# A hybrid decoder layer: TensorE's order stated by hand too, transfers in the account of outstanding work, the solve's tiles in another pool, three short products ahead of the branch projections

## The chip, the cores and the metric

The kernel runs on one core of a Trainium2 chip. The metric is the device time of one execution in microseconds (us). Engine names as in the profile: PE is TensorE's matmul, PEld its weight load, DVE VectorE, ACT ScalarE, POOL GpSimd, SP the engine that issues the weights' transfers.

## The reference, cut to what matters

One decoder layer on a sequence of 256 positions of width 2048, all in float32, eight heads of 128 in each of two branches, and a gated feed-forward part of width 5632.

```python
h = rms_norm(x, ln1)
proj = h @ w_in                     # q, k, v, beta, decay, z of A; q, k, v of B; two gates
y_a = gated_deltanet(...) @ w_branch_a       # causal conv 4, l2norm, chunks of 64,
                                             # triangular solve per chunk, state scan, norm
y_b = moba_attention(rope(q_b), rope(k_b), v_b) @ w_branch_b   # block 256: causal attention here
merged = sigmoid(gate_a) * y_a + sigmoid(gate_b) * y_b
x = x + merged @ w_out
h = rms_norm(x, ln2)
u = causal_dwconv(h @ w_up, ffn_conv, ffn_conv_bias)           # width 3
u_gate, u_val = split(u)
x = x + (silu(u_gate) * u_val) @ w_down
out = rms_norm(x, final_norm)
```

## The kernel before

Activations lie transposed, 128 features on the partitions and 256 positions in a row. Each large product is made of three: a value is split into a high and a low part of a reduced float32 type, and for each block of 128 input features TensorE multiplies `wh` by the high part, `wh` by the low part and `wl` by the high part. That triple, of 256 columns each, is what `block` writes through `main_mm` (L168). A piece of weights comes by a transfer of 1 MB into `wraw`; ScalarE casts 1024 columns of it to `wh`, VectorE subtracts to get `wl`. Such 1024 columns are called a half here: 24 products. Four buffers of halves are there, and halves are counted from the start of the program: the gates' projections (`ps_gate`) lie in halves 112 to 175, the branches (`ps_br`) in 176 to 207, the output projection (`ps_wo`) in 208 to 239, the up projection (`ps_up`) from 240, the down projection (`pd`) behind 416.

Beside the large products of the input projection run the two branches, written as generators ("jobs"): `decay`, the gated DeltaNet with its triangular solve, the rotary part and the attention. Each time 1700 ns worth of large products have been written (16 products), `main_mm` calls `tick()`, which lets each job go on to its next `yield` if an account of outstanding work permits it: `Metered` adds a number for each operation that it issues on ScalarE and VectorE to `load`, a tick takes `EVERY` off, no job steps while `load` is above `ROOM`, and `ready` holds a job back until its last operations should be done. What has to wait longer says `yield from wait(n)`, a fixed number of ticks. `quick` holds the jobs of the projections' own results, `bg` the background ones.

From the first projection on, `manual_schedule` states that DVE, ACT and POOL take their instructions in the order in which they are written. TensorE is not among them: its order is put together by a scheduler with a model of its own. `order_st.close()` ends the stated order behind the gates.

Names that return below: `posi` and `ang` (positions and angles), `cs`, `dS`, `CS` (cosines and sines and their way through DRAM), `X_` and `Xc` (the rotated quarter of queries and keys, fetched by POOL's transfers), `sc` and `s_` (scores), `pT` (transposed weights of the attention); in the DeltaNet `ssq`, `pvt`, `dA`, `X`, `Xa`, `tm`, `W`, `Xr` (the solve), `py`, `Y`, `pu`, `r`, `w`, `z`, `g`, `po`, `pot` (short products behind it, of 128 columns and less). `g` is the pool of the solve's tiles, on the right side of the memory; it is freed when `early` has four entries, and the gates' results take its place. `gl` is the pool of what lives longer. A `kick` (L275) is three dummy products of 128 columns ahead of a chunk, named in `KICKS`.

Of the kernel before, what the change touches and what calls it, by code (L numbers as in the profile page):

```python
# [11 lines left out]
F32 = mybir.dt.float32  # L12
# [18 lines left out]
TABLE = 1220  # L31
TABLES = (AF.Exp, AF.Sigmoid, AF.Silu, AF.Sqrt, AF.Sin)
# [3 lines left out]
KICKS = {"gate": (7,), "up": (1, 23)}  # L36
# [39 lines left out]
def layer_kernel(ctx: ExitStack, tc: tile.TileContext, w_first, xT, pos, cst, vec, convw, ffw, bdv,  # L76
                 w_gdn, w_bd, w_moba, w_mv, w_gate, w_ba, w_bb, w_o, w_up, w_dn, fnorm, out):
    nc = tc.nc
    pe, pool, sp = nc.tensor, nc.gpsimd, nc.sync

    class Metered:
# [5 lines left out]
        def __getattr__(self, op):  # L87
            f = getattr(self.eng, op)

            def run(*args, **kw):  # L90
                n = max([a.free_size() for a in (*args, *kw.values()) if hasattr(a, "free_size")], default=0)
                if op == "reciprocal":
                    n *= 6
                if op == "dma_start":
                    n = 0
                func = [a for a in (*args, *kw.values()) if isinstance(a, type(AF.Exp)) and a in TABLES]
                extra = TABLE if func and func[0] != self.table else 0
                self.table = func[0] if func else self.table
                met(self.name, n * self.per + self.each, extra)
                return f(*args, **kw)  # L100

            return run

    act, dve = Metered(nc.scalar, "act", 0.87, 110), Metered(nc.vector, "dve", 1.03, 60)
# [13 lines left out]
    quick, bg, load, clock, ready = [], [], {"dve": 0.0, "act": 0.0}, [0.0], {}  # L118
# [147 lines left out]
    def chunk(x, kt, name, steps=((0, 0, None), (1, 0, None)), c=None):  # L266
        ps = mmt("ps_" + name)
        ws = {}
        if kt == H:
            ws = dict.fromkeys(range(2), take())  # L270
        if c in KICKS.get(name, ()):
            ws[0] = take()
            idle = sdt("kick")
            for _ in range(3):
                pe.matmul(idle[:, :P], ws[0][1][0][0][:, :P], x.one(0, 0)[:, :P], start=True, stop=True)  # L275
# [155 lines left out]
    gl_st = ExitStack()  # L431
    gl = gl_st.enter_context(tc.tile_pool(name="gl", bufs=2, reuse_waits="tile"))
# [3 lines left out]
    dr = gdn_st.enter_context(tc.tile_pool(name="dr", bufs=2, space=bass.MemoryType.DRAM))  # L436
# [3 lines left out]
    def rotary():  # L440
        while not left:
            yield
        posi = m.tile([P, 32], I32, name="posi", tag="pT_")
        sp.dma_start(posi, pos)
        ang = m.tile([P, 32], F32, name="ang", tag="s_")
        with late():
            dve.tensor_copy(ang, posi)
        dve.tensor_scalar(ang, ang, C["invf"], None, op0=ALU.mult)
        qn = m.tile([P, 32], F32, name="qn", tag="s_")
        MAGIC = 1.5 * 2 ** 23  # L450

# [36 lines left out]
        dve.tensor_scalar(ang, ang, 3.1415925, -3.1415925, op0=ALU.min, op1=ALU.max)  # L488
        cs = m.tile([P, 2, 32], F32, name="cs_", tag="s_")
        act.activation(cs[:, 1], ang, AF.Sin)  # L490
        act.activation(cs[:, 0], ang, AF.Sin, scale=0.5)
        yield
        dve.tensor_tensor(cs[:, 0], cs[:, 0], cs[:, 0], op=ALU.mult)
        dve.tensor_scalar(cs[:, 0], cs[:, 0], -2.0, 1.0, op0=ALU.mult, op1=ALU.add)
        for a in range(2):
            for j in range(2):
                pool.dma_start(dram(dS, a * 32 * T + j * T, (2 * T, 16), (1, T)), cs[:, a])
        yield from wait(2)
        for a in range(2):
            pool.dma_start(CS[:, a], dram(dS, a * 32 * T, (0, 2), (P, 64), (1, P)))  # L500
        turned.append(True)


    def decay():
# [38 lines left out]
        dve.tensor_scalar(rem, gc[:, :P], gc[:, P - 1:P], -1.0, op0=ALU.subtract, op1=ALU.mult)  # L543
        left.append(rem)
# [18 lines left out]
    left, early, ended, joined, turned, seen = [], [], [], [], [], []  # L563
# [57 lines left out]
    def gdn(h0, kq, v):  # L621
# [53 lines left out]
        yield from wait(2)  # L675
# [19 lines left out]
        yield  # L695
        vb = gl.tile([P, 2, 2, P], F32, name="vb")
# [12 lines left out]
        yield from wait(2)  # L709
# [4 lines left out]
        yield from wait(2)  # L714
# [3 lines left out]
        for i in range(1, 16):  # L718
            tm = g.tile([P, 2, 2, 16], F32, name="tm", tag="tm", bufs=1)
# [15 lines left out]
        def rows(dst, w, a, neg):  # L735
            tm = g.tile([P, 2, 16, 16], F32, name="tw", tag="tm", bufs=1)
# [4 lines left out]
        W = g.tile([P, 2, 16], F32, name="W", bufs=1)  # L741
        rows(W, X0, r3(Xa[:, :512], 32)[:, :, 16:], True)
        yield
        Xr = g.tile([P, 16, 16], F32, name="Xr", bufs=1)
        pool.dma_start(Xr.rearrange("p m c -> p (m c)"), dram(dX, 0, (256, 16), (0, 8), (1, 256)))
        yield from wait(5)
# [6 lines left out]
        yield from wait(2)  # L753
# [7 lines left out]
        yield from wait(2)  # L761
# [5 lines left out]
        yield from wait(2)  # L767
        Et = gl.tile([P, 2, 32], F32, name="Et", bufs=1)
        dve.transpose(Et, E[:, 0])
        yield from wait(2)  # L770
# [8 lines left out]
        yield from wait(2)  # L779
# [3 lines left out]
        yield  # L783
        for j in range(2):
# [10 lines left out]
        for i in range(2):  # L795
# [11 lines left out]
            yield from wait(2)  # L807
# [5 lines left out]
            if i == 0:  # L813
# [8 lines left out]
                yield from wait(2)  # L822
# [19 lines left out]
        yield from wait(2)  # L842
# [8 lines left out]
    def moba(h0, q, k, v):  # L851
# [12 lines left out]
        yield from wait(4)  # L864
# [6 lines left out]
        yield from wait(4)  # L871
# [35 lines left out]
        yield from wait(2)  # L907
# [3 lines left out]
        yield from wait(2)  # L911
# [13 lines left out]
        yield from wait(2)  # L925
# [16 lines left out]
    def delta(gr):  # L942
# [5 lines left out]
        if gr == 0:  # L948
            order_st.enter_context(tc.manual_schedule(engines={
                mybir.EngineType.DVE, mybir.EngineType.Activation, mybir.EngineType.Pool}))  # L950
            load.update(dve=2400.0, act=0.0)
# [80 lines left out]
    while len(early) < 4:  # L1032
        tick()
# [3 lines left out]
    more = gp.tile([P, 14, 2, T], F32, name="gts")  # L1037
    gts += [more[:, c] for c in range(14)]
# [229 lines left out]
```

## Time and profile before

| | us |
|---|---|
| three runs: lowest, median, highest | 1468.44, 1473.16, 1473.19 |
| the profiled execution | 1473.24 |
| its span | 1471.4 |
| PE, DVE, ACT, POOL busy | 1449.4, 963.4, 767.0, 187.1 |
| idle of DVE just ahead of `wl` | 379.8 |
| idle of ACT just ahead of `wh` | 559.9 |

The execution lasts 1.8 us longer than the span that the profile covers. The profile cuts the span into stages by time: the input projection with the two branches beside it lies from the start to about 485, the remaining gates to 563, the branch projections to 654, the output projection to 744, the up projection to 1224 and the down projection behind it. A row's releaser is the operation that ended the wait. Products overlap in the records, so the duration of a single one (0.28 us alone) is longer than the distance between two; the distance is read from a stretch of many in the chain of work.

### The profile page before, as it was taken

The page shows a single profiled execution, that of the slowest core. Times are in us where ns is not written, and L with a number is a line of the kernel's source. Part 1 is how long each engine was busy: PE and PEld are TensorE (multiplying, and loading weights), DVE is VectorE, ACT ScalarE, POOL GpSimd, SP SyncE. Part 2 cuts the span into 40 slices and gives each one's busy share as a digit, 9 for nine tenths or more (in the row PEclk, how much of TensorE's full clock was granted, in tenths as well). Part 3 has the DMA queues.
Part 4 walks back from the last instruction along what each step waited for, and adds up shares of the span by engine and source line. Part 5 has one row for each costly group of instructions (what it writes and reads, how often), then busy time and mean ns, then how long its engine had stood idle before and what let it go on. Part 6 is the DMA issues. An engine that isn't in the chain of part 4 may idle for free.

```text
span 1471.4 us, 26958 instructions
## 1 busy us (share of the span) xinstructions
PE 1449.4 (99%) x11268; PEld 1390.0 (94%) x11268; DVE 963.4 (65%) x1385; ACT 767.0 (52%) x1093; POOL 187.1 (13%) x236
## 2 busy tenths in 40 slices
PE   9998999999999999999999999999999999999998
PEld 9988899999999999999999999999999998888886
DVE  7785869686755645766776666666666666644454
ACT  7654556656565544444555554545555554444444
POOL 0003131223210300100131111111111110000000
PEclk9999999999999999999999999999999999999999
DMA  8555565656355555566586555555555555555553
GB/s 310 173 180 160 178 207 184 203 172 224 126 190 178 184 190 183 181 220 205 196 246 216 197 201 192 187 196 200 191 188 196 201 188 185 200 200 192 186 195 114
DMA packets 46457, 283.80 MB, mean 193 GB/s; under 512 B 7632, under 2 KB 8800, under 8 KB 14464
## 3 DMA queue, kind: packets, MB, share of 16 engines
q1 hardware_dynamic: 39344, 270.38, 53.1%
q0 software_dynamic: 6272, 9.61, 2.5%
q8 instruction: 88, 1.44, 0.4%
q10 hardware_dynamic: 720, 2.10, 0.4%
q14 instruction: 33, 0.27, 0.1%
HBM read 275.34 MB, written 3.82 MB: 190 GB/s over the span
## 4 chain that ended last, share of the span: by engine, by line
PE 93%; DVE 3%; ACT 2%; DMA 1%; issue 1%; POOL 0%; ACTq 0%; DVEq 0%; POOLq 0%
PE ps_up L168 33%; PE pd L116 16%; PE ps_gate L168 12%; PE ps_wo L168 6%; PE ps_br L168 6%; PE ps_gdn L168 6%; PE ps_moba L168 5%; PE ps_v L168 2%; PE ps_z L168 2%; PE ps_gdn L341 2%; DVE wl L100 1%; ACT wh L100 1%; ACT L100 0%; PE g L116 0%; DMA dS<-cs__1202 0%
## 5 line engine op out<-in xcount | busy, mean ns | idle before, releaser
L100 DVE TENSOR_TENSOR wl<-wraw,wh 128x1024 fp32r<-128x1024 f32 (+1 forms) x496 | 612.6, 1238 | 379.8 <-ACT wh L100 378.7
L100 ACT CAST wh<-wraw 128x1024 fp32r<-128x1024 f32 (+1 forms) x496 | 514.5, 1042 | 559.9 <-PE ps_up L168 195.5
L168 PE MATMUL ps_up<-h,wh 128*128 128x256 f32 x2816 | 479.5, 276 | 0.0
L168 PEld LDWEIGHTS ps_up<-h,wh 128*128 128x128 f32 x2816 | 424.1, 188 | 0.0
L168 PE MATMUL ps_up<-h,wl 128*128 128x256 f32 x1408 | 389.2, 276 | 0.0
L168 PEld LDWEIGHTS ps_up<-h,wl 128*128 128x128 f32 x1408 | 264.3, 188 | 0.0
L168 PE MATMUL ps_gate<-hc,wh 128*128 128x256 f32 x1024 | 181.7, 281 | 1.5 <-ACT wh L100 1.5
L168 PEld LDWEIGHTS ps_gate<-hc,wh 128*128 128x128 f32 x1024 | 156.4, 189 | 1.9 <-ACT wh L100 1.9
L168 PE MATMUL ps_gate<-hc,wl 128*128 128x256 f32 x512 | 143.4, 280 | 1.9 <-DVE wl L100 1.9
L116 PE MATMUL pd<-wl,ah 128*128 128x512 f32 x336 | 125.5, 389 | 0.0
L116 PE MATMUL pd<-wh,al 128*128 128x512 f32 x336 | 124.4, 389 | 0.0
L116 PE MATMUL pd<-wh,ah 128*128 128x512 f32 x336 | 115.6, 389 | 0.0
L168 PE MATMUL ps_gdn<-hc,wh 128*128 128x256 f32 x640 | 115.0, 283 | 0.0
L1132 POOL TENSOR_TENSOR acts<-sg,cvf 128x256 f32<-128x256 f32 x44 | 62.7, 1426 | 408.3 <-ACT sg L100 400.0
L168 PEld LDWEIGHTS ps_gdn<-hc,wh 128*128 128x128 f32 x640 | 99.5, 192 | 0.5 <-issue 0.4
L168 PEld LDWEIGHTS ps_gate<-hc,wl 128*128 128x128 f32 x512 | 96.1, 188 | 2.3 <-DVE wl L100 2.3
L168 PE MATMUL ps_gdn<-hc,wl 128*128 128x256 f32 x320 | 91.0, 286 | 6.5 <-DVE wl L100 6.5
L168 PE MATMUL ps_moba<-hc,wh 128*128 128x256 f32 x512 | 90.2, 279 | 2.3 <-ACT wh L100 2.3
L168 PE MATMUL ps_wo<-mc,wh 128*128 128x256 f32 x512 | 90.5, 281 | 0.0
L168 PEld LDWEIGHTS ps_moba<-hc,wh 128*128 128x128 f32 x512 | 77.6, 188 | 2.6 <-ACT wh L100 2.5
L168 PEld LDWEIGHTS ps_wo<-mc,wh 128*128 128x128 f32 x512 | 78.6, 190 | 0.0
L116 PEld LDWEIGHTS pd<-wh,ah 128*128 128x128 f32 x336 | 63.1, 188 | 13.1
(405 smaller groups left out, 1981.8 us busy)
## 6 DMA issues: line engine op xcount, KB each, us to landing
wraw<-in_w_up SPq DMA_DIRECT2D x88, 1024.0 KB, 4.9
wraw<-in_w_dn SPq DMA_DIRECT2D x44, 1024.0 KB, 4.9
wraw<-in_w_gate SPq DMA_DIRECT2D x32, 1024.0 KB, 4.9
wraw<-in_w_gdn SPq DMA_DIRECT2D x28, 1024.0 KB, 5.2
wraw<-in_w_moba SPq DMA_DIRECT2D x16, 1024.0 KB, 4.9
wraw<-in_w_o SPq DMA_DIRECT2D x16, 1024.0 KB, 4.9
wraw<-in_w_mv SPq DMA_DIRECT2D x8, 1024.0 KB, 5.0
wraw<-in_w_ba SPq DMA_DIRECT2D x8, 1024.0 KB, 4.8
```

What stands on the lines that cost most here:

```text
L100: return f(*args, **kw)
L116: pe.matmul(ps, a, b, start=(start and i == 0), stop=(stop and i == n - 1), **kw)
L168: mark[0] = pe.matmul(ps, a, b, start=start, stop=stop, skip_group_check=True).ins
L341: pe.matmul(ps_two[b // 2][:, b % 2], wv[t][:, k - a, b * P:(b + 1) * P], hc.one(k, x_), start=(k == t == x_ == b % 2 == 0), stop=(k == KD ...
L1132: pool.tensor_tensor(acts[:, c, :], sg, t[:, 1, :], op=ALU.mult)
```

## The change

It has four parts. TensorE joins the engines whose order is the written one, and the stated order ends behind the last gates. POOL gets an account too (`Metered`, `ISSUE` = 560 for each transfer), and `yield "land"` stands where a job waits for a transfer: its next step is not taken ahead of the clock plus POOL's account plus `LAND` = 5200. A tick is still gated by DVE and ACT alone. Several waits become a single `yield`; the load of `posi` is issued by POOL, no longer by SP. The solve's tiles (`X`, `Xa`, `tm`, `W`, `Xr`) and the DRAM pool go to `gl`; `g` is freed when `clear` has four entries, behind the transposes `pvt`. The gates' results are split: eleven in the place of `g`, three in a pool `gq` that opens when `gl` and `m` are closed. And a kick stands ahead of the first branch chunk.

```diff
+ISSUE = 560
+MORE = 11
+LAND = 5200
-KICKS = {"gate": (7,), "up": (1, 23)}
+KICKS = {"gate": (7,), "br": (0,), "up": (1, 23)}
...
-                    n = 0
+                    n = ISSUE
...
+    pool = Metered(nc.gpsimd, "pool", 1.0, 0)
...
+    def landed():
+        return clock[0] + load["pool"] + LAND
+
     def step(jobs, it):
         old = dict(load)
-        if next(it, bg) is bg:
+        said = next(it, bg)
+        if said is bg:
             jobs.remove(it)
-        ready[id(it)] = clock[0] + max([load[e] for e in load if load[e] > old[e]], default=0.0)
+        ready[id(it)] = clock[0] + max([load[e] for e in ("dve", "act") if load[e] > old[e]], default=0.0)
+        if said == "land":
+            ready[id(it)] = max(ready[id(it)], landed())
...
-                if max(load.values()) < most and ready.get(id(it), 0.0) <= clock[0] + soon_:
+                if max(load["dve"], load["act"]) < most and ready.get(id(it), 0.0) <= clock[0] + soon_:
...
         if c in KICKS.get(name, ()):
-            ws[0] = take()
+            ws[0] = ws.get(0) or take()
...
-        sp.dma_start(posi, pos)
+        pool.dma_start(posi, pos)
+        yield "land"
...
-        yield from wait(2)
+        yield "land"
         for a in range(2):
             pool.dma_start(CS[:, a], dram(dS, a * 32 * T, (0, 2), (P, 64), (1, P)))
...
+        clear.append(h0)
...
+        while 2 * len(early) < h0:
+            yield
-        X = g.tile([P, 160], F32, name="X", bufs=1)
+        X = gl.tile([P, 160], F32, name="X", bufs=1)
         pool.tensor_copy(X, C["rows"])
-        yield from wait(2)
+        yield "land"
...
-        Xa = g.tile([P, 33 * 32], F32, name="Xa", bufs=1)
+        Xa = gl.tile([P, 33 * 32], F32, name="Xa", bufs=1)
         pool.dma_start(Xa[:, :1024], dram(dC, 0, (1024, 16), (0, 8), (1, 1024)))
-        yield from wait(4)
+        yield "land"
...
-        yield from wait(2)
+        there = landed()
         py = r3(sdt("py")[:, :64], 32)
...
+        while clock[0] < there:
+            yield
...
         each(lambda t, b, o: pool.dma_start(X_[o, b], t))
-        yield from wait(4)
+        yield "land"
...
         each(lambda t, b, o: pool.dma_start(t, Xc[o, b]))
-        yield from wait(4)
+        yield "land"
...
             order_st.enter_context(tc.manual_schedule(engines={
-                mybir.EngineType.DVE, mybir.EngineType.Activation, mybir.EngineType.Pool}))
+                mybir.EngineType.DVE, mybir.EngineType.Activation, mybir.EngineType.Pool,
+                mybir.EngineType.PE}))
...
-    while len(early) < 4:
+    while len(clear) < 4:
         tick()
     gdn_st.close()
...
-    for c in range(2, 16):
+    for c in range(2, 2 + MORE):
         gate(c, gts[c])
     while quick or bg:
         tick()
-    order_st.close()
     m_st.close()
     gl_st.close()
+    gq = y_st.enter_context(tc.tile_pool(name="gq", bufs=1, side="right", reuse_waits="tile"))
+    last = gq.tile([P, 14 - MORE, 2, T], F32, name="gtl")
+    gts += [last[:, c] for c in range(14 - MORE)]
+    for c in range(2 + MORE, 16):
+        gate(c, gts[c])
+    flushed(quick)
+    order_st.close()
...
-        join(bts[0], chunk(yc[0], H, "br"), gts[c])
+        join(bts[0], chunk(yc[0], H, "br", c=2 * c), gts[c])
```

Three places of the resulting order. First VectorE around the first rotation. `cs` is the last step of the cosines and sines, whose transfers `Xc` depends on; `un` and `kq` are steps of a projection's own convolution; each `wl` is one half. Before:

```order
L100 TENSOR_TENSOR cs__1202<-cs__1202 128x32
L100 TENSOR_SCALAR cs__1202<-cs__1202 128x32
L100 SCALAR_TENSOR_TENSOR aq_1226<-g_1119,st,gam 128x256 x2
L100 TENSOR_TENSOR wl<-wraw,wh 128x1024 x4
L100 TENSOR_TENSOR Xc<-X__1308,CS 128x256
L100 TENSOR_TENSOR Xs<-X__1308,CS 128x128 x2
L100 TENSOR_TENSOR Xc<-Xc,Xs 128x128 x2
L100 TENSOR_TENSOR un<-ps_gdn,R_415 128x512
L100 TENSOR_TENSOR wl<-wraw,wh 128x1024 x2
```

Now, from `cs` on, the first rows, and behind them the rows up to `Xc`, with five more `wl` in between:

```order
L103 TENSOR_TENSOR cs__1358<-cs__1358 128x32
L103 TENSOR_SCALAR cs__1358<-cs__1358 128x32
L103 TENSOR_TENSOR un<-ps_gdn,R_415 128x512
L103 TENSOR_TENSOR wl<-wraw,wh 128x1024 x2
L103 SCALAR_TENSOR_TENSOR kq<-un,cwv,kq 128x255
```

```order
L103 SCALAR_TENSOR_TENSOR kq<-un,cwv,kq 128x253
L103 TENSOR_TENSOR wl<-wraw,wh 128x1024
L103 TENSOR_TENSOR Xc<-X__1289,CS 128x256
L103 TENSOR_TENSOR Xs<-X__1289,CS 128x128 x2
L103 TENSOR_TENSOR Xc<-Xc,Xs 128x128 x2
```

Between `cs` and `Xc` stood four `wl`, now eight, and `un` has moved from behind `Xc` to the place right behind `cs`. The scores' products `sc` of this job stood in TensorE's row at half 42.04, with their first reader on VectorE ahead of the `wl` of half 42; now at half 47.33, with the reader ahead of the `wl` of half 51.

Second, TensorE around the last `pot`, the DeltaNet's last short product, in the gates. Before, at half 147.33:

```order
L168 MATMUL ps_gate<-hc,wl 128x256
L168 MATMUL ps_gate<-hc,wh 128x256 x2
L846 MATMUL pot<-ct,ot 128x128 x4
L168 MATMUL ps_gate<-hc,wl 128x256
L168 MATMUL ps_gate<-hc,wh 128x256 x2
```

Now, at half 150.67:

```order
L178 MATMUL ps_gate<-hc,wl 128x256
L178 MATMUL ps_gate<-hc,wh 128x256
L862 MATMUL pot<-ct,ot 128x128 x4
L178 MATMUL ps_gate<-hc,wh 128x256
L178 MATMUL ps_gate<-hc,wl 128x256
```

`pot` has moved down by three and a third halves, and it stands behind one `wh` product of its triple where it stood behind two.

Third, a short product with its operand, as the changed order has them: TensorE around `pu`, at half 64.00, and VectorE around `Y`, which `pu` reads. The `wl` rows ahead of and behind `Y` are those of halves 66 and 67.

```order
L178 MATMUL ps_gdn<-hc,wh 128x256 x2
L178 MATMUL ps_gdn<-hc,wl 128x256
L796 MATMUL pu<-E,Y 128x32 x2
L178 MATMUL ps_gdn<-hc,wh 128x256 x2
L178 MATMUL ps_gdn<-hc,wl 128x256
```

```order
L103 TENSOR_TENSOR wl<-wraw,wh 128x1024
L103 TENSOR_TENSOR Y<-py,ct 128x256
L103 TENSOR_TENSOR s__2528<-sc,ct 128x384
L103 TENSOR_REDUCE mx<-s__2528 128x1 x2
L103 TENSOR_SCALAR mx<-mx 128x2
L103 TENSOR_TENSOR un<-ps_gdn,R_415 128x512
L103 TENSOR_TENSOR wl<-wraw,wh 128x1024
```

In the changed order such short products stand only where a tick was, that is at multiples of 16 products, two thirds of a half.

More of the change, by code (lines that the diff above doesn't have):

```diff
@@ L78, in layer_kernel @@
     nc = tc.nc
-    pe, pool, sp = nc.tensor, nc.gpsimd, nc.sync
+    pe, sp = nc.tensor, nc.sync
     class Metered:
@@ L116, in mmg @@
             pe.matmul(ps, a, b, start=(start and i == 0), stop=(stop and i == n - 1), **kw)
-    quick, bg, load, clock, ready = [], [], {"dve": 0.0, "act": 0.0}, [0.0], {}
+    quick, bg, load, clock, ready = [], [], {"dve": 0.0, "act": 0.0, "pool": 0.0}, [0.0], {}
     def met(name, n, more=0.0):
         load[name] += n + more
+    def landed():
+        return clock[0] + load["pool"] + LAND
     def step(jobs, it):
         old = dict(load)
-        if next(it, bg) is bg:
+        said = next(it, bg)
+        if said is bg:
             jobs.remove(it)
-        ready[id(it)] = clock[0] + max([load[e] for e in load if load[e] > old[e]], default=0.0)
+        ready[id(it)] = clock[0] + max([load[e] for e in ("dve", "act") if load[e] > old[e]], default=0.0)
+        if said == "land":
+            ready[id(it)] = max(ready[id(it)], landed())
     def tick():
@@ L431, in layer_kernel @@
     gl_st = ExitStack()
+    dr = gl_st.enter_context(tc.tile_pool(name="dr", bufs=2, space=bass.MemoryType.DRAM))
     gl = gl_st.enter_context(tc.tile_pool(name="gl", bufs=2, reuse_waits="tile"))
@@ L435, in layer_kernel @@
     gdn_st = ExitStack()
-    dr = gdn_st.enter_context(tc.tile_pool(name="dr", bufs=2, space=bass.MemoryType.DRAM))
     g = gdn_st.enter_context(tc.tile_pool(name="g", bufs=2, side="right", reuse_waits="tile"))
@@ L561, in turned_out @@
         dve.tensor_scalar(cols[:, 0:2, :].rearrange("p a b -> p (a b)"), pt[:, :32], -1.0, None, op0=ALU.mult)
-    left, early, ended, joined, turned, seen = [], [], [], [], [], []
+    left, early, ended, joined, turned, seen, clear = [], [], [], [], [], [], []
     order_st = ExitStack()
@@ L708, in gdn @@
             pool.dma_start(dC[8 * e:8 * e + 8], dram(dA, e * 32 * (P + 1), (64 * (P + 1), 8), (P, 32), (1, 32)))
-        yield from wait(2)
-        Xa = g.tile([P, 33 * 32], F32, name="Xa", bufs=1)
+        yield "land"
+        Xa = gl.tile([P, 33 * 32], F32, name="Xa", bufs=1)
         pool.dma_start(Xa[:, :1024], dram(dC, 0, (1024, 16), (0, 8), (1, 1024)))
-        yield from wait(4)
+        yield "land"
         pool.memset(r3(Xa, 33)[:, :, 0:1], -1.0)
-        yield from wait(2)
+        yield
         Xd = X.rearrange("p (e x) -> p e x", e=2)[:, :, :64].rearrange(
@@ L718, in gdn @@
         for i in range(1, 16):
-            tm = g.tile([P, 2, 2, 16], F32, name="tm", tag="tm", bufs=1)
+            tm = gl.tile([P, 2, 2, 16], F32, name="tm", tag="tm", bufs=1)
             dve.tensor_tensor(tm[:, :, :, :i + 1], Xd[:, :, :, :i + 1],
@@ L735, in rows @@
         def rows(dst, w, a, neg):
-            tm = g.tile([P, 2, 16, 16], F32, name="tw", tag="tm", bufs=1)
+            tm = gl.tile([P, 2, 16, 16], F32, name="tw", tag="tm", bufs=1)
             dve.tensor_tensor(tm, w[:, :, None, :].to_broadcast([P, 2, 16, 16]),
@@ L739, in rows @@
             dve.tensor_reduce(dst, tm, axis=AX.X, op=ALU.add, negate=neg)
-        W = g.tile([P, 2, 16], F32, name="W", bufs=1)
+        W = gl.tile([P, 2, 16], F32, name="W", bufs=1)
         rows(W, X0, r3(Xa[:, :512], 32)[:, :, 16:], True)
-        yield
-        Xr = g.tile([P, 16, 16], F32, name="Xr", bufs=1)
+        yield "land"
+        Xr = gl.tile([P, 16, 16], F32, name="Xr", bufs=1)
         pool.dma_start(Xr.rearrange("p m c -> p (m c)"), dram(dX, 0, (256, 16), (0, 8), (1, 256)))
-        yield from wait(5)
+        yield "land"
         rows(Xm, W, Xr, False)
@@ L752, in gdn @@
         early.append(h0)
-        yield from wait(2)
+        yield "land"
         E = gl.tile([P, 2, 2, 32], F32, name="E", bufs=1)
@@ L760, in gdn @@
                            dram(dA, j * (P + 1) * P + 64, (P, 64), (2 * (P + 1) * P, 2), (1, 64)))
-        yield from wait(2)
+        yield "land"
+        Et = gl.tile([P, 2, 32], F32, name="Et", bufs=1)
+        dve.transpose(Et, E[:, 0])
         for b in range(2):
@@ L766, in gdn @@
             yield
[L767 to L770, printed above, removed]
+        there = landed()
         py = r3(sdt("py")[:, :64], 32)
@@ L778, in gdn @@
                           r3(C["mb"], 32)[:, None].to_broadcast([P, 2, 4, 32]), op=ALU.mult)
-        yield from wait(2)
+        yield
         pu = r3(sdt("pu")[:, :64], 32)
@@ L783, in gdn @@
         yield
+        while clock[0] < there:
+            yield
         for j in range(2):
@@ L806, in gdn @@
             dve.tensor_tensor(vb[:, i, 1], vb[:, i, 1], pz, op=ALU.subtract)
-            yield from wait(2)
+            yield
             p1_ = sdt("w1")[:, :P]
@@ L821, in gdn @@
                         dve.tensor_tensor(vb[o, 1, b], vb[o, 1, b], pr[64 * b:64 * b + 64, j, :], op=ALU.subtract)
-                yield from wait(2)
+                yield
         ended.append(h0)
@@ L841, in gdn @@
             act.mul(ot[:, p], po[:, p], st[:, 7, p:p + 1])
-        yield from wait(2)
+        yield
         pot = r3(sdt("pot"), T)
@@ L863, in moba @@
         each(lambda t, b, o: pool.dma_start(X_[o, b], t))
-        yield from wait(4)
+        yield "land"
         dve.tensor_tensor(Xc, X_, CS[:, 0:1, :].to_broadcast([P, 2, P]), op=ALU.mult)
@@ L870, in moba @@
         each(lambda t, b, o: pool.dma_start(t, Xc[o, b]))
-        yield from wait(4)
+        yield "land"
         ss, pss, mxs = [], [], []
@@ L906, in moba @@
         exps(1)
-        yield from wait(2)
+        yield
         share(0)
@@ L910, in moba @@
         share(1)
-        yield from wait(2)
+        yield
         pps = []
@@ L924, in moba @@
             ss[j] = pT
-        yield from wait(2)
+        yield
         py = r3(sdt("py_b"), T)
@@ L949, in delta @@
             order_st.enter_context(tc.manual_schedule(engines={
-                mybir.EngineType.DVE, mybir.EngineType.Activation, mybir.EngineType.Pool}))
-            load.update(dve=2400.0, act=0.0)
+                mybir.EngineType.DVE, mybir.EngineType.Activation, mybir.EngineType.Pool,
+                mybir.EngineType.PE}))
+            load.update(dve=2400.0, act=0.0, pool=0.0)
             bg.append(decay())
@@ L1036, in layer_kernel @@
     gp = y_st.enter_context(tc.tile_pool(name="gp", bufs=1, side="right", reuse_waits="tile"))
-    more = gp.tile([P, 14, 2, T], F32, name="gts")
-    gts += [more[:, c] for c in range(14)]
-    for c in range(2, 16):
+    more = gp.tile([P, MORE, 2, T], F32, name="gts")
+    gts += [more[:, c] for c in range(MORE)]
+    for c in range(2, 2 + MORE):
         gate(c, gts[c])
```

## The prediction

> **What bounds the kernel now.** I read the page first, for the engines' shares of the span. Quoted are the span and the busy times (us, share of the span, instructions).
>
> ```profile
> span 1471.4 us, 26958 instructions
> PE 1449.4 (99%) x11268; PEld 1390.0 (94%) x11268; DVE 963.4 (65%) x1385; ACT 767.0 (52%) x1093; POOL 187.1 (13%) x236
> ```
>
> TensorE is busy for 1449.4 of 1471.4 us, and the change takes no product out of it. So there are two kinds of gain: the 22 us in which it is not busy, and the time that its own products take. The view of busy time by stretches finds both; its columns are the stretch, its length, then busy time and instructions of PE, PEld, DVE, ACT and POOL, the granted clock, the DMA share and GB/s.
>
> ```profile
> 60.00:100.00 40.00, 39.68 (x253) 34.20 (x252) 33.33 (x76) 24.33 (x32) 1.46 (x2) 1.00 0.49 165
> 100.00:165.00 65.00, 55.77 (x420) 53.83 (x419) 46.01 (x104) 32.84 (x51) 16.31 (x28) 0.92 0.52 167
> 165.00:395.00 230.00, 229.01 (x1874) 222.12 (x1873) 176.54 (x358) 140.92 (x254) 58.50 (x105) 1.00 0.58 192
> 395.00:415.00 20.00, 16.62 (x135) 15.71 (x134) 10.17 (x20) 12.96 (x30) 7.32 (x13) 1.00 0.36 115
> ```
>
> TensorE idles 0.32, 9.23, 0.99 and 3.38 us in these four, 13.9 us together, nearly all of it at 100 to 165 and 395 to 415. Only in the second is the granted clock below 1.00. What it waits for comes from the view of waits (us in total, times, longest), of TensorE in 100 to 165, in 395 to 415, and one row of 165 to 480; then of VectorE in 60 to 480.
>
> ```profile
> PE ps_gdn L168 <- DVE wl L100: 6.5, 5, 3.0
> PE ps_moba L168 <- ACT wh L100: 2.3, 1, 2.3
> ...
> PE ps_gate L168 <- DVE wl L100: 1.9, 2, 1.1
> PE ps_gate L168 <- ACT wh L100: 1.5, 2, 1.2
> ...
> PE pT L916 <- DVE s__2575 L100: 0.7, 1, 0.7
> ```
>
> ```profile
> DVE Xc L100 <- DMA X__1308<-qk: 7.6, 1, 7.6
> DVE s__4831 L100 <- PE sc L876: 6.9, 1, 6.9
> DVE s__1521 L100 <- PE sc L876: 6.5, 1, 6.5
> ...
> DVE ang L100 <- DMA posi<-in_pos: 2.7, 1, 2.7
> ```
>
> TensorE waits for weight tiles, not for results: nearly always it is a `wl` or a `wh` that is late. They are late because VectorE itself stood in three long waits with their subtractions queued behind: 7.6 us for a rotary transfer (`Xc`), and twice 6.5 to 6.9 us for the scores `sc`, which TensorE had in its own row later than VectorE expected them. VectorE and ScalarE have time to spare otherwise.
>
> ```profile
> L100 DVE TENSOR_TENSOR wl<-wraw,wh 128x1024 fp32r<-128x1024 f32 (+1 forms) x496 | 612.6, 1238 | 379.8 <-ACT wh L100 378.7
> L100 ACT CAST wh<-wraw 128x1024 fp32r<-128x1024 f32 (+1 forms) x496 | 514.5, 1042 | 559.9 <-PE ps_up L168 195.5
> ```
>
> A half (1024 weight columns, 24 products) costs 1.04 us of cast and then 1.24 us of subtraction (last columns: mean ns).
>
> The products' own time comes from the chain of work that ended last (start, us, group). Two stretches of it, 365 to 382 and from 440 on:
>
> ```profile
> 370.34 9.53 PE ps_gate L168 x84
> ...
> 446.53 5.66 PE ps_gate L168 x48
> ...
> 468.12 13.73 PE ps_gate L168 x121
> 481.85 0.44 PE pot L846 x4
> 482.29 81.03 PE ps_gate L168 x688
> 563.32 90.45 PE ps_br L168 x768
> 653.77 90.45 PE ps_wo L168 x768
> 744.23 8.36 PE ps_up L168 x71
> ...
> 753.02 2.94 PE ps_up L168 x25
> 755.97 0.28 PE kick L275 x3
> 756.25 239.43 PE ps_up L168 x2112
> ```
>
> One product of 256 columns takes 9.53/84 = 113.5 ns in some groups and 81.03/688 = 117.8 ns in others, with no wait between. It is a state: 117.8 ns sets in after `pot` at 481.85 and lasts through 1632 products and a small group, up to the kick, three dummy products of 128 columns. From there 239.43/2112 = 113.4 ns holds for 2112.
>
> **The change, part by part.**
>
> (1) *Stalls, −22.8 us.* The order stated for TensorE puts `sc` into its row where the job reaches it, the same position from which the other engines' rows are written, and the job goes on only after the account says that the transfers have landed. In the order of the changed kernel `Xc` stands eight `wl` behind `cs` on VectorE, before it four; the next `un` stands ahead of it, no longer behind. Before, the transfer landed 7.6 us too late. Four more halves are 4 × 24 × 0.1134 = 10.9 us, so the wait is gone with 3.3 us to spare, if VectorE isn't faster elsewhere. `sc` stands 3.67 halves (10.0 us) ahead of the subtraction that waits for its reader (before: 0.04 halves behind), at 121 similarly. What goes with these waits is the 13.9 us of idle; then the slow clock, and the restarts:
>
> ```profile
> 126.75 0.58 PE L168 MATMUL ps_gdn<-hc,wl 128*128 128x256 f32 x1 [2.97 <-DVE wl L100]
> 127.13 0.63 PE L168 MATMUL ps_gdn<-hc,wh 128*128 128x256 f32 x2
> ```
>
> After the wait of 2.97 us (timeline: start, us) two products take 0.63 us and not 0.39 us: the clock is halved, (1 − 0.92) × 65 = 5.2 us in all. About eleven waits also restart TensorE. The row of `126.75` lasts 0.3 us more than the 0.28 us that such a product takes alone; with 0.34 us each I put 3.7 us. Together 13.9 + 5.2 + 3.7 = 22.8.
>
> (2) *New waits of short products, +8.4 us.* Now a short product stands in the row at the tick at which it was written, and TensorE can't pass it. There are some 55 such places behind half 60. Where its operand is made on VectorE, it is ready when VectorE has got that far. VectorE may run ahead by what four buffers of a half allow: `wl` of half n+3 starts once TensorE has left half n−1. At `pu` (half 64.00 ← `Y`, which stands between the `wl` of 66 and 67) the `wl` of 66 can be done 2.28 us after TensorE leaves half 62 (1.04 + 1.24); the half between takes 24 × 0.1134 = 2.72 us, so that is 0.44 us ahead of `pu`, and `Y` with its own time behind it is just late. Twelve places have a margin of this size (`pu` 64, `pT` 70, `r` 72, `w` and `g` 76, `pot` 82, `r` 98, `ssq` 100, `w` 102, `r` 120, `z` 138, `po` 146 or their neighbours); the rest have more. No such place is in the trace of before. Below, each costs nothing, and 12 × 0 = 0; above, the longest wait for a cast, 2.3 us, gives 12 × 2.3 = 27.6. The nearest row is the one short product that waited in its row, `pT` for VectorE: 0.7 us. I take 12 × 0.7 = 8.4.
>
> (3) *The kick before the branches, −6.8 us.* The slow products behind half 176 take 90.45 + 90.45 + 8.36 + 2.94 = 192.2 us; 1632 × 0.1134 = 185.1. That saves 7.1 us, less 0.28 us for the three dummies. That the kick works there is read from the one at 755.97. It stands at the beginning of a half, as the new one does, and the slow products of `ps_br` are of the same shape.
>
> (4) *The last gates, −3.0 us.* After `pot` the order now has the remaining products of a k-block differently cut. In these two stretches of the timeline the same group of four stands once behind one `wh` product of a triple and once behind two:
>
> ```profile
> 369.61 0.28 PE L168 MATMUL ps_gate<-hc,wh 128*128 128x256 f32 x1
> 369.73 0.61 PE L816 MATMUL r<-u,aq 128*128 128x128 f32 x4
> ```
>
> ```profile
> 445.69 0.39 PE L168 MATMUL ps_gate<-hc,wh 128*128 128x256 f32 x2
> 445.92 0.61 PE L816 MATMUL r<-u,aq 128*128 128x128 f32 x4
> ```
>
> The first is followed by the 9.53/84 = 113.5 ns, the second by 5.66/48 = 117.9 ns. `pot` stood behind two, now it stands behind one. 688 × 0.1134 = 78.0 instead of 81.03. Its price lies between 0 and −3.0 (the state may come out the same); I take −3.0, by the nearer row, the first.
>
> (5) *Costed at nothing.* `posi` moves from SP's queue to POOL's. POOL is busy for 13% of the span, and the transfer's reader is one job with no product behind it for tens of us; if that cover went, VectorE would stand as now, 2.7 us. The solve's tiles in the late pool remove a release and add none on TensorE's path; the gates' wait moves from the solve to the transposes, ahead of the place where `wh` and `s__4831` piled up at 395. Two table loads less on ScalarE (52% busy) are hidden by the products. If POOL's dearer account only slowed the jobs, they would still end at half 151 of 176; 25 halves (68 us) are left.
>
> The sum is −22.8 + 8.4 − 6.8 − 3.0 = −24.2. The profiled execution took 1473.24 us for a span of 1471.4, 1.8 around it, and the median shown is 1473.16, so they agree. 1471.4 − 24.2 + 1.8 = **1449.0 us**.
>
> [...]
>
> **The rivals.**
>
> *B. The kick or the phase doesn't set the rate.* For it: the state's origin isn't visible, and (3) rests on three kicks, (4) on a cut that I know only from short stretches. Against it: the switch at 755.97 comes with the kick and stays for 2112 products. Without (3): 1449.0 + 6.8 = 1455.8; without (4) as well, 1458.8.
>
> *C. Waits move rather than vanish.* The twelve tight places cost 1.5 us each, halfway between the two rows of (2), so 18.0 us instead of 8.4: 1458.6. At the upper end, 27.6, it is 1468.2. For it: VectorE's lead shrinks whenever TensorE speeds up. Against it: 379.8 us of idle on VectorE.
>
> *D. The change doesn't do it.* `Xc` waits still: the rotary goes through two chained transfers on POOL behind the solve's, and all jobs step later. Then nothing of (1) comes, and (2) to (4) remain: 1473.2 + 8.4 − 6.8 − 3.0 = 1471.8, not to be told from before.
>
> *E. Slower.* One mechanism: with its order stated TensorE takes nothing forward past a short product whose operand isn't there. At each of the 55 places behind half 60 it stands in line for VectorE, ScalarE or a transfer, and `wl` and `wh` gain nothing from it since their buffers are full. All gains together are 32.6 us, so it decides from 32.6/55 = 0.6 us a place on. At 0.9 us, a little over the 0.7 us row, 49.5 − 32.6 gives 1473.2 + 16.9 = 1490. For it: the 0.7 us row is longer than this bound. Against it: in before 73 such places had one such wait, and in the new order only 12 are tight.
>
> [...]
>
> **How the numbers follow.** Chances: forecast 0.48 (1441 to 1456 with the bound of (2) at 0 and of (4) at 0), B 0.18, C 0.18, D 0.08, E 0.08. A measurement of this kernel can tell about 0.5%, 7.4 us, from no change: faster means below 1465.8, slower above 1480.5. Forecast, B and most of C lie below: 0.84. D is no change, 0.08; E is slower, 0.08. For 8 in 10 the range takes the forecast, B, and C up to about 2.0 us a place (24 us, 1464.6, rounded down): 1440 to 1463; C's upper end, D and E stay outside.
>
> **What would show it.** Right: no wait of VectorE for `X_` or `sc` over 1 us before 480; the granted clock 1.00 from 60 to 1224; `ps_br` and `ps_wo` at 768 × 0.1134 = 87.1 us each; the last 600-odd gate products at 113.4 ns; the idle left behind some short products, below 1 us each. Wrong: `ps_br` still at 90.45 us (B); TensorE's idle over 20 us, in front of `pu`, `r`, `w`, `pT` (C, or E with over 40 us and a halved clock behind a wait near 3 us); a wait for `X_` as long as before (D).

## The result, and the profile after

| | us |
|---|---|
| before, median of four runs | 1471.70 |
| after, median of four runs (lowest, highest) | 1463.05 (1462.90, 1463.61) |
| ratio after to before, 95% interval | 0.9945 [0.9925, 0.9964] |
| the profiled execution after, its span | 1462.9, 1461.1 |

The change makes the kernel 8.7 us faster, where 24.2 were forecast; 1463.05 lies just outside the range. The spans of the two profiled executions differ by 10.3 us.

Busy time of the changed kernel by stretches, with the columns of the prediction:

```profile
60.00:100.00 40.00, 39.22 (x251) 34.41 (x250) 31.93 (x51) 22.48 (x26) 2.00 (x3) 1.00 0.64 214
100.00:165.00 65.00, 63.27 (x542) 62.10 (x540) 55.59 (x133) 42.13 (x66) 16.68 (x28) 1.00 0.57 187
165.00:395.00 230.00, 219.23 (x1730) 211.19 (x1731) 169.35 (x350) 130.34 (x238) 57.24 (x104) 0.98 0.54 180
395.00:415.00 20.00, 20.00 (x175) 19.95 (x174) 14.05 (x26) 13.20 (x26) 0.00 (x0) 1.00 0.47 165
415.00:485.00 70.00, 69.76 (x602) 69.45 (x601) 35.24 (x42) 38.20 (x69) 7.32 (x13) 1.00 0.50 170
```

TensorE's idle has left 100 to 165 (9.23 us before, 1.73 now) and 395 to 415 (3.38, now 0). It stands in 165 to 395 instead: 10.77 us, before 0.99. All five together have 13.52 us where they had 13.92. The slow clock has moved too: the second row has 1.00, the third 0.98. Three narrow stretches show where that comes from (the granted clock is the third number from the end):

```profile
168.00:172.00 4.00, 4.00 (x15) 3.44 (x16) 2.28 (x6) 0.48 (x1) 0.00 (x0) 0.57 0.80 262
226.00:230.00 4.00, 4.00 (x22) 4.00 (x23) 3.76 (x12) 0.00 (x0) 0.00 (x0) 0.57 0.19 76
386.00:391.00 5.00, 4.47 (x25) 4.44 (x26) 2.69 (x10) 1.14 (x2) 1.74 (x4) 0.66 0.72 249
```

Each loses its length times what its clock lacks to 1.00, together 0.43 × 4 + 0.43 × 4 + 0.34 × 5 = 5.1 us; the kernel before lost 5.2 us in 100 to 165. So the stalls as a whole gave some 0.5 us.

TensorE's waits in the changed kernel (in total, times, longest), and VectorE's one wait for a rotary transfer:

```profile
PE w L825 <- DVE vb L103: 5.4, 3, 3.3
PE pT L932 <- DVE s__2557 L103: 2.0, 1, 2.0
PE pT L932 <- DVE s__1922 L103: 1.8, 1, 1.8
PE pT L932 <- DVE s__1863 L103: 1.8, 1, 1.8
...
PE pT L932 <- DVE s__2528 L103: 0.9, 1, 0.9
...
PE w L813 <- DVE vb L103: 0.2, 1, 0.2
```

```profile
DVE Xc L103 <- DMA X__4152<-qk: 0.2, 1, 0.2
```

VectorE no longer waits for `sc` or for a transfer to speak of, and TensorE waits for `wl` 1.3 us in all. It now waits for results: eight short products, `pT` and `w`, stand in its row ahead of what they read, 12.1 us in all.

The chain from the last `pot` on:

```profile
490.73 68.92 PE ps_gate L178 x608
559.66 0.28 PE kick L285 x3
559.94 87.11 PE ps_br L178 x768
647.04 87.04 PE ps_wo L178 x768
734.08 8.05 PE ps_up L178 x71
...
742.56 2.94 PE ps_up L178 x25
```

Gates, branches and output projection all run at 113.4 ns a product (68.92/608, 87.11/768). The last four groups of products take 185.14 us where they took 192.2, and 608 gate products save 608 × 4.4 ns = 2.7 us. With the kick's 0.28 us that is −9.5, and with the stalls' −0.5 it is −10.0, for a difference of the spans of −10.3. **Nearly all of the gain is the rate; the stalls were only exchanged.**

### The profile page after: what moved, and what is told of

Same layout as the page of the kernel before. It is cut to its first block, busy times and chain, and to the rows that moved or that the text cites. A ratio compares the mean times of both kernels' runs of the same rounds, so it can differ in the third digit from the quotient of the medians.

```text
span 1461.1 us, 26969 instructions
## 1 busy us (share of the span) xinstructions
PE 1439.3 (99%) x11271; PEld 1380.7 (94%) x11271; DVE 964.5 (66%) x1385; ACT 766.2 (52%) x1091; POOL 186.0 (13%) x237
## 4 chain that ended last, share of the span: by engine, by line
PE 92%; DVE 5%; ACT 2%; issue 1%; POOL 0%; DVEq 0%; ACTq 0%; POOLq 0%
PE ps_up L178 33%; PE pd L120 16%; PE ps_gate L178 11%; PE ps_gdn L178 6%; PE ps_br L178 6%; PE ps_wo L178 6%; PE ps_moba L178 5%; PE ps_v L178 3%; DVE wl L103 2%; PE ps_gdn L351 2%; PE ps_z L178 1%; ACT wh L103 1%; PE g L120 1%; DVE tm L103 0%; DVE X L103 0%
## 5 line engine op out<-in xcount | busy, mean ns | idle before, releaser
L178 PE MATMUL ps_gdn<-hc,wh 128*128 128x256 f32 x640 | 111.9, 279 | 0.0
L178 PE MATMUL ps_wo<-mc,wh 128*128 128x256 f32 x512 | 87.1, 276 | 0.0
L120 PEld LDWEIGHTS pd<-wh,al 128*128 128x128 f32 x336 | 63.1, 188 | 13.1
```

Source lines behind the costliest of these rows:

```text
L120: pe.matmul(ps, a, b, start=(start and i == 0), stop=(stop and i == n - 1), **kw)
L178: mark[0] = pe.matmul(ps, a, b, start=start, stop=stop, skip_group_check=True).ins
```

## The experiments

Each was timed beside runs of the kernel before on its chip, whose median was 1470.1 to 1473.6 us; the ratio to before has its 95% interval, and theories M and N are those of the expectations. Differences to the changed kernel or between runs can go across chips, on which the kernel before itself differs by up to 3.5 us; differences of 2 or 3 us there are uncertain.

**x1, two ticks at `pT` and `w`.**

```diff
         share(1)
-        yield
+        yield from wait(2)
         pps = []
...
             dve.tensor_tensor(vb[:, i, 1], vb[:, i, 1], pz, op=ALU.subtract)
-            yield
+            yield from wait(2)
             p1_ = sdt("w1")[:, :P]
```

> The changed kernel, with the wait ahead of pT's transposes and the wait ahead of the w product that reads vb set back from one tick to two. Theory M (the account of outstanding work runs ahead of VectorE by more than a tick, so a product that stands one tick behind the operation it reads waits): TensorE's idle in 165 to 395 falls from 10.8 us to below 4, its granted clock there from 0.98 to 1.00 (4.6 us), and the time from 1463.05 to 1450-1455. Theory N (with its order stated TensorE waits at some short product anyway): the waits turn up at the next short products, and the time stays within 3 us of 1463.

1452.88 us, ratio 0.9873 [0.9858, 0.9887], 10.2 us below the changed kernel. Busy time of this run in the stretch in question:

```profile
165.00:395.00 230.00, 225.43 (x1817) 217.57 (x1818) 175.42 (x365) 138.28 (x252) 58.41 (x104) 1.00 0.56 186
```

The idle falls from 10.77 to 4.57 us, a little above the 4 of theory M, and the clock is whole again, 5.1 us. In the time and the clock M holds. Some two fifths of the idle are left, mostly at other short products (`sc` 1.4 us, one `w` 1.3 us).

**y2 and y3, the two ticks at `pT` alone and at `w` alone.** The diffs are the two halves of the one above.

> The changed kernel with two ticks ahead of pT's transposes alone. Theory M: the 6.5 us of pT's waits go and the slow clock behind them (some 2 us), while w's 5.4 us stay: 1463 to 1454-1457. Theory N (waits move): under 3 us of gain.

> The changed kernel with two ticks ahead of the w product that reads vb alone. Theory M: w's 5.4 us and the slow clock behind the longest (some 2 us) go, pT's 6.5 us stay: 1456-1459. Theory N: under 3 us of gain.

y2: 1461.51 us, 0.9934 [0.9916, 0.9951]. y3: 1461.23 us, 0.9931 [0.9910, 0.9952]. Each alone gives under 2 us, together they give 10.2: N's number came out each time, its mechanism only in y2. In y2 the waits of `pT` are gone, and those of `w` have grown from 5.4 us:

```profile
PE w L825 <- DVE vb L103: 8.6, 4, 3.3
```

The new one, of 3.15 us, stands in the timeline of y2 from 221 us on, right behind the place of `pT`. So a wait can move to the next product whose operand lies behind the same pile of work on VectorE. In y3 no wait moved: those of `w` are gone and `pT` is as it was. Its idle in 165 to 395 is 5.87 us, 4.9 less, but the gates behind `pot` ran slow in its profiled execution (67.84 us for 576 products, 117.8 ns), which takes 2.5 us back; without that, y3 would have gained an estimated 4.3 us (1.8 + 2.5).

In neither did the clock recover. The slow stretches of y2 and then of y3:

```profile
225.00:230.00 5.00, 5.00 (x32) 5.00 (x31) 4.69 (x14) 2.85 (x6) 0.00 (x0) 0.66 0.45 152
382.00:390.00 8.00, 6.38 (x29) 6.26 (x30) 6.43 (x16) 2.52 (x5) 2.84 (x5) 0.57 0.73 261
```

```profile
166.00:175.00 9.00, 7.16 (x34) 6.57 (x34) 4.09 (x11) 1.06 (x3) 0.00 (x0) 0.62 0.34 117
228.00:232.00 4.00, 4.00 (x23) 4.00 (x23) 3.73 (x12) 0.00 (x0) 0.00 (x0) 0.57 0.03 8
```

Each pair loses 5.1 us, as much as the changed kernel. Half of x1's gain is this clock, and it came back only when the waits of both kinds were gone.

**z4, the solve's steps charged as they cost.**

```diff
             dve.tensor_reduce(Xd[:, :, :, i], tm[:, :, :, :i + 1], axis=AX.X, op=ALU.add, negate=True)
+            met("dve", 260.0)
```

> The changed kernel, TensorE's order stated, waits of one tick; each of the solve's fifteen steps is charged 260 more to VectorE's account (a pair of tm and X takes 0.46 us on VectorE, the account has about 0.2). Theory M' (the products wait because the account has VectorE further on than it is): the waits of pT and w fall from 11.9 to below 5 us, 1453-1457. If the lack of a tick at these places counts and not the account: they stay, 1460-1464.

1448.42 us, 0.9837 [0.9815, 0.9859], 14.6 us below the changed kernel and below the 1453 to 1457 of theory M', with TensorE's order stated and every wait of one tick. TensorE's waits for `pT` and `w` in this run:

```profile
PE pT L933 <- DVE s__1925 L103: 0.6, 1, 0.6
...
PE pT L933 <- DVE s__2571 L103: 0.4, 1, 0.4
```

From 11.9 us they fall to 1.0. Why they came is read in the changed kernel's timeline of VectorE ahead of the longest of them, `w` at half 118.67, where TensorE stands from 383.3 us on:

```profile
381.86 0.68 DVE L103 TENSOR_TENSOR gt<-ps_gate,R 128x512 f32<-128x512 f32 x1
382.46 2.35 DVE L103 TENSOR_TENSOR wl<-wraw,wh 128x1024 fp32r<-128x1024 f32 x2
384.73 0.24 DVE L103 TENSOR_TENSOR tm<-X,Xa 128x52 f32<-128x52 f32 x1
385.00 0.21 DVE L103 TENSOR_REDUCE X<-tm 128x4 f32<-128x52 f32 x1
385.24 0.25 DVE L103 TENSOR_TENSOR tm<-X,Xa 128x56 f32<-128x56 f32 x1
...
386.20 0.28 DVE L103 TENSOR_TENSOR vb<-vb,z 128x128 f32<-128x128 f32 x1
```

```profile
386.53 0.49 PE L825 MATMUL w<-vb,UB 128*128 128x128 f32 x2 [3.25 <-DVE vb L103]
```

VectorE isn't idle there; it works without a gap through what was written ahead of `vb`. One pair of `tm` and `X` takes 385.24 − 384.73 = 0.51 us, and the account charges 1.03 × 52 + 60 = 114 ns for each of the two, 0.23 us. Three pairs stand at a tick, so the account has VectorE 0.8 us further on than it is after each, and the jobs' next products are written too early by it. That is a quarter of this wait of 3.25 us; that such errors add up over several ticks is argued, and borne out only by the fall from 11.9 to 1.0. The error is there at every width: a `tm` of 8 columns takes 165 ns in the changed kernel and one of 64 takes 266 (means of four each), where the account has 68 and 126.

The charge also lets the jobs end later (the last `pot` stands at half 156.67 and not 150.67), so other neighbours changed as well; x1 took most of the same waits away by another means. A charge of the same size at another place was not tried, so it is not shown whether the account's error at the solve counts or a slower pace of the jobs.

**x2, TensorE's order left to the scheduler.**

```diff
-                mybir.EngineType.DVE, mybir.EngineType.Activation, mybir.EngineType.Pool,
-                mybir.EngineType.PE}))
+                mybir.EngineType.DVE, mybir.EngineType.Activation, mybir.EngineType.Pool}))
```

> The changed kernel with TensorE's order left to the scheduler. If the stated order brought the waits of pT and w, these go (idle in 165 to 395 from 10.8 us to about 1); if it also removed the waits of VectorE for sc (6.5 and 6.9 us before), those return. Theory M: waits for sc return at one or two places, for X_ not (the account has that), so idle of 4 to 8 us and 1455-1463. Theory N: TensorE free is better altogether, 1448-1453.

1447.41 us, 0.9833 [0.9817, 0.9850], 15.6 us below the changed kernel. Of the waits of `pT` and `w` one of 0.5 us is left, and VectorE waits for `sc` once, 2.2 us. The time is just below N's number, and it shows that the sc waits of before were not a matter of TensorE's order alone: with the jobs placed later by the account the scheduler places `sc` in time.

**y4, both.** Two ticks as in x1, and the scheduler as in x2.

> Both at once: two ticks at pT and w, and TensorE's order left to the scheduler. Theory M: the scheduler can place pT and w where their operands are there, so the two ticks have nothing left to remove: 1447.4 plus or minus 2. If the few waits left in that run (pT 0.5, wl 2.4 us) come from the same shortage: 1443-1446.

1447.59 us, 0.9840 [0.9823, 0.9857]. The ticks have nothing left to remove.

**v1, the charge and the scheduler.** z4's line and x2's.

> The solve charged as in z4, and TensorE's order left to the scheduler as in x2. If both remove the same waits (short products that stand ahead of their operands): no more to gain, 1446-1449. If the scheduler also removes others: 1442-1445.

1444.53 us, 0.9819 [0.9806, 0.9832], the fastest of all, 18.5 us below the changed kernel, though its interval overlaps that of x2. Its TensorE idles 0.5 us in all from 60 to 485, where it idles 3.5 us in z4 and 3.7 us in x2, so here the two removed different waits.

**x4, TensorE's order stated, nothing else.** The kernel before with this engine added to the list.

> The kernel before with nothing but TensorE added to the engines whose order is stated; the waits keep their two ticks. Theory M: VectorE's waits for sc go, its wait for X_ (7.6 us) stays; short products wait little: idle of 4 to 9 us in 100 to 415, 1462-1468. Theory N: new waits at the short products take more than the sc waits gave: 1475 or more.

1467.83 us, 0.9979 [0.9964, 0.9994], ten executions from 1464.25 to 1473.71. VectorE's waits for `sc` fall to 1.5 and 0.6 us, its wait for `X_` stays, and TensorE waits itself:

```profile
DVE Xc L100 <- DMA X__1308<-qk: 6.2, 1, 6.2
```

```profile
PE sc L875 <- DMA qk<-Xc: 11.1, 3, 8.2
PE g L116 <- DVE kql L100: 3.6, 1, 3.6
```

Where VectorE waited for `sc`, TensorE now stands in front of `sc` itself, until the transfers behind the late `Xc` have landed. TensorE's idle in 100 to 415 is 13.4 us, more than the 4 to 9 of theory M and as much as before (13.6); 60 to 100 has 4.2 us more than before. The time lies in M's range only because the gates, `ps_br` and `ps_wo` ran at 113.4 ns in its profiled execution (77.99, 87.04 and 87.04 us), without a kick. By the stated order alone nothing was gained in stalls.

**z2, no time for a transfer to land.** x2 with `LAND = 0`.

> TensorE's order left to the scheduler as in x2, LAND = 0: a job waiting for a transfer is held back by POOL's account alone. If the 5200 are what removed VectorE's wait for X_ (7.6 us before): waits of VectorE or POOL for transfers return, idle of 8 us or more, 1455-1470. If the scheduler or POOL's account did it: 1447-1450.

1494.76 us, 1.0148 [1.0129, 1.0168]. VectorE's waits in 60 to 500:

```profile
DVE Et L103 <- DMA E<-dE: 14.2, 4, 8.1
DVE tm L103 <- POOL Xa L103: 11.9, 3, 8.3
DVE Xc L103 <- DMA X__1306<-qk: 8.0, 1, 8.0
```

This costs 47.4 us against x2, more than expected: in the changed code the 5200 replaced the old waits of several ticks at every transfer of the solve too. So z2 has neither the old waits nor the new one, and 47.4 us is not what the 5200 gained over the kernel before. Of the change's parts this one carries the stalls.

**z1, the gates' place freed at the end of the solves again.** x2 with `len(early)` for `len(clear)` ahead of `gdn_st.close()`.

> TensorE's order left to the scheduler as in x2, and g freed only when the four solves are done (len(early)) as before. If the freeing at the transposes is what took the idle of 395 to 415 away (3.4 us before, there behind ticks without products): this idle returns and the time is 1451-1454. If the account of transfers did it alone: 1447.4 plus or minus 1.5.

1453.28 us, 0.9867 [0.9848, 0.9886], 5.9 us above x2 (5.0 by the two ratios). The idle in 395 to 415 comes back to 1.07 us, not to 3.4, and in x2 it is none; the larger part of the difference is another thing. From the chain of z1:

```profile
461.28 89.16 PE ps_gate L178 x757
```

These are 117.8 ns a product; x2 has 113.4 ns behind its last `pot` (68.95 us for 608). That alone is 757 × 4.4 ns = 3.3 us. What the freeing is worth is therefore at most some 2.6 us.

**x3, the kick alone.** The kernel before with the `KICKS` entry and the two lines that it needs.

> The kernel before with nothing but the kick ahead of the first branch chunk. If the kick sets the rate: ps_br and ps_wo 87.1 us each for 90.45, all in all 6.8 us faster than before. If the changed phase of the gates did it: ps_br and ps_wo stay at 90.45 and the time is that of before.

1464.29 us, 0.9949 [0.9934, 0.9964], 7.45 us below before; `ps_br` 87.11, `ps_wo` 87.04 us, and the gates ahead of it still 81.03. Ahead of the kick 117.8 ns, behind it 113.4: the kick sets the rate, as forecast.

**y1, the changed kernel without its kick.**

```diff
-KICKS = {"gate": (7,), "br": (0,), "up": (1, 23)}
+KICKS = {"gate": (7,), "up": (1, 23)}
```

> The changed kernel without the kick ahead of the branches. If the kick is needed each time: ps_br and ps_wo 90.45 us each and 6.8 us more, about 1470. If the rate is a state that lasts until something irregular comes (in the changed kernel the gates behind the last pot already run at 113.4 ns): ps_br and ps_wo stay at 87.1, and the time is that of the changed kernel less 0.3 us.

Neither. Ten executions fell into two groups: seven from 1462.11 to 1464.49, three from 1471.86 to 1472.81. The profiled one is of the first, with 87.04 us each for `ps_br` and `ps_wo`. The groups' medians lie 9.9 us apart, and the 608 + 1632 products from the last `pot` to the next kick at 117.8 for 113.4 ns make 2240 × 4.4 ns = 9.9 us. No execution of the slower group was profiled; that it is the rate is inferred from this agreement.

**v2, the new kick moved to gate chunk 10**, 24 halves earlier and just behind the last `pot`.

```diff
-KICKS = {"gate": (7,), "br": (0,), "up": (1, 23)}
+KICKS = {"gate": (7, 10), "up": (1, 23)}
```

> The changed kernel with its new kick moved from the first branch chunk to gate chunk 10, behind the last pot. If the rate behind pot is a matter of chance in each execution and a kick makes it 113.4 ns wherever it stands: all executions within 1.5 us of 1463, none near 1472 (without the kick 3 of 10 were). If the kick has to stand at the branches: some executions at 1470-1473.

1463.83 us, 0.9952 [0.9939, 0.9964]; six executions from 1463.08 to 1465.48, a little wider than expected, and none near 1472. That fits a kick that settles the rate wherever it stands, but doesn't show it: the gates ran fast already ahead of this kick in the profiled execution (3.64 us for 32 products), and at y1's 7 in 10 six fast executions would come by luck in 0.7⁶, about 12 of 100 cases.

**z3, x2 with a further kick at gate chunk 10.**

> x2 with one more kick, ahead of gate chunk 10, the first behind the last pot. If the rate behind pot falls one way or the other by chance: runs in which the 600-odd gates behind pot run slow lose up to 2.4 us less; median 1446-1447.5 and a smaller spread. If the gates there are fast in all runs of x2: 0.3 us slower.

1446.83 us, 0.9826 [0.9807, 0.9845], not to be told from x2, and the spread is not smaller (2.3 us, in x2 1.4).

## Why the prediction was wrong

**(1) Stalls, −22.8: right in the mechanism, some 4 us too large.** VectorE's waits for `sc` are gone, the one for `X_` is 0.2 us, the idle and the slow clock of 100 to 165 and of 395 to 415 have left. Of the 13.52 us of idle in the changed kernel all but 1.4 belong to (2), so (1) took away 12.5 us of idle and 5.2 us of slow clock. The 3.7 us for eleven restarts were counted in part twice: the row that they were read from, at 126.75, lies in the stretch of the halved clock. At the full clock the first product behind a wait is 0.1 us longer than the 0.28 us of one alone, as in this row of the kernel before:

```profile
140.98 0.39 PE L168 MATMUL ps_gdn<-hc,wl 128*128 128x256 f32 x1 [1.86 <-DVE wl L100]
```

That makes 1.1 us for eleven, and (1) some 18.8. What removed the waits is above all the account of transfers and not the stated order: x2 has it without the order but for one wait for `sc` of 2.2 us, z2 loses it without the 5200, and x4, the order alone, leaves VectorE's wait for `X_` at 6.2 us and puts TensorE itself in front of `sc`.

**(2) New waits of short products, +8.4: this step failed.** It measured 12.1 us of waits and 5.1 us of slow clock behind them, 17.2 in all, and took back what (1) gave. These 8.8 us and the 4 of (1) are most of the 14 us by which the forecast missed. Two errors lie in it. The first is the list of twelve places. It was read from the order on the supposition that VectorE runs ahead by as much as four buffers permit. Of the eight waits three are on the list (`pT` at 70, twice, and `w` at 102: 3.9 us), and ten of the twelve places have no wait in the view; a small one (`w` at 142, 0.2 us) lies between two of the list. The dearer four (`pT` at 53.33, twice 1.8 us, `w` at 96.67 and 118.67: 8.1 us) have more room by the order, but VectorE stood behind a pile of work of which the account misses a part (z4). The change had also cut the waits at just these places from two ticks to one, which no step of the prediction priced; x1 shows what that cost, 10.2 us. The second error is the price: 0.7 us was the only wait in its row, and the real ones were up to 3.3 us, with half the clock behind three of the places, for which the sum had no term.

**(3) The kick, −6.8: right in size** (192.2 to 185.14 us, less 0.28), and x3 shows that the kick does it from the slow rate. In the changed kernel that is partly luck: the gates ahead of the kick ran at 113.4 ns already, and without it 7 executions of 10 had the same time (y1).

**(4) The gates, −3.0: right in size (−2.7) by luck, wrong in its reason.** The cut of the triple decides nothing here. In x4 the last `pot` stands behind two `wh` products at half 147.33, just as before, and the rate behind it is the fast one; in x1 and y3 `pot` stands at half 152.00 both times, and the rates differ. The chains of x4, x1 and y3, in this order:

```profile
485.03 77.99 PE ps_gate L168 x688
```

```profile
484.11 65.30 PE ps_gate L178 x576
```

```profile
489.76 67.84 PE ps_gate L178 x576
```

These are 113.4, 113.4 and 117.8 ns.

**(5) At nothing: right,** as far as `posi` and the pools go. No wait for `posi` is left, and the new account lets the jobs end three halves later, without cost.

**The rivals.** C is what happened: the waits moved from VectorE's row into TensorE's. Its price of 1458.6 to 1468.2 holds the time, though it was made from waits without the slow clock behind them; the range was to take C in up to 1464.6, but was closed at 1463. E's mechanism was there too, at eight places and not 55. D is refuted by VectorE's waits. B's times did not come, and x3 speaks against it for the kick; but that the phase doesn't set the rate, the other half of B, came out under (4).

What stays open: what in TensorE makes the rate, and why the kernel before runs at the slow one behind `pot` (in its own profile and in x3's, and none of its executions took less than 1468.0 us), the changed one mostly at the fast one.

## What to carry to other kernels

With TensorE's order stated by hand its short products waited in its row for what they read, 12.1 us here; leave the engine that bounds the kernel to the scheduler (x2, 15.6 us faster), or calibrate the model first on the small operations, for which the charge by size was too low (0.23 us for a pair of `tm` and `X` that takes 0.51). Read the room of a product from the consuming and the producing engine's timelines, not from the order. And when one wait goes, look at the next product in line behind the same pile before counting the gain: two half measures gave under 2 us each, and both together 10, because the clock, 5.1 us, came back only with both.

## What the runs showed of the hardware

TensorE's rate for one and the same stream of products was one of two in these chains, 113.4 or 117.8 ns at a granted clock of 1.00. Which it was after a group of short products differed between runs with the same neighbours (the chains under (4)) and, by the times of y1, between executions of one program (7 to 3). Three dummy products of 128 columns stand between the slow rate and the fast one ahead of the branches in x3, y3 and z1 (gates at 117.8 ns, then `ps_br` at 113.4), and ahead of the kick's chunk of the up projection in the kernel before (117.8 ns, then 113.4 for 2112 products). Behind the kicks at these two places the chains of all runs but v1, whose chain is not among them, show the fast rate: 87.11 us for the 768 products of `ps_br`, 239.43 or 239.44 us for the 2112 of `ps_up`.

Stretches at half the clock stand behind waits of TensorE shorter than 3 us. In the changed kernel they follow the two at half 53.33 (1.83 and 1.84 us) and the two at 70 (0.94 and 1.96 us): the granted clock is 0.57 from 168 to 172 and from 226 to 230. In x2 a single wait of 1.98 us comes ahead of one, as the two products in 0.63 us show, which take 0.39 us at the full clock:

```profile
330.81 0.38 PE L178 MATMUL ps_moba<-hc,wl 128*128 128x256 f32 x1 [1.98 <-DVE wl L103]
...
332.30 0.63 PE L178 MATMUL ps_moba<-hc,wh 128*128 128x256 f32 x2
```

The wait of 1.86 us at 140.98 in the kernel before, shown under (1), was not followed by such a stretch (granted clock 1.00 from 140 to 156). So the length of a single wait doesn't decide in these runs. In the clock's own records of the kernel before and the changed one the slow stretches ahead of the last 5 us last 3.41 us, one of them 6.83, and in the changed kernel the three begin 58.03 and 160.43 us apart, 17 and 47 times 3.413. In the 3.41 us ahead of each of them TensorE stood idle for 2.4, 2.3 and 3.0 us. Of the wait of 1.86 us such a step holds 1.4 us at most. Counted in such steps from 60 to 480 us, the two traces have five steps at the full clock with 2.1 to 3.0 us of idle, each with a slow one behind it; the other steps at the full clock have 1.4 us at most, and none of them has a slow one behind it. So the idle time within a fixed step of 3.41 us fits these two traces; at which share of it between these the clock falls was not tested.
